# Six small loads move from SP's DMA queue to ACT's at the start of a one-core hybrid S5, DeltaNet and expert block

## The chip, the cores and the metric

The kernel runs on one core of a Trainium2 chip. Its time is the device time of one execution in microseconds (us), the median of several runs.

The engines that matter here are TensorE (PE in the rows, its weight loads PEld), VectorE (DVE), ScalarE (ACT), GpSimd (POOL) and SyncE (SP), which only issues DMAs. Each of them executes its own list of instructions in order. ACT issues DMAs as well, from the same list as its arithmetic. The issuing instructions have rows of their own, marked SPq or ACTq.

## What is computed

One block of a diffusion backbone, for 256 latent tokens `x` and 256 context tokens `ctx` of width 1024, in float32. In short:

```
mod   = silu(c) @ w_mod + b_mod          # the same with c_ctx for the context
h     = rmsnorm(x) * norm1 * (1 + scale) + shift
u, qkv, gate, b, a, br = split(h @ w_in)
yA    = S5(u)          # complex diagonal scan, lam_re, lam_im, log_step, b, c
yB    = GatedDeltaNet(silu(short_conv(qkv)), gate, b, a)
x     = x + gate1 * ((sig(br0) * yA @ w_a + sig(br1) * yB @ w_b) @ w_out)
x     = x + gate2 * experts(h2)          # top 4 of 32 clamped-SwiGLU experts, 12 MB each
out   = rmsnorm(x)
```

Of S5 the part that the change touches is the discretisation, which needs three short vectors:

```
dt  = exp(log_step);  mag = exp(lam_re * dt)
ar, ai = mag * cos(lam_im * dt), mag * sin(lam_im * dt)
fr, fi = ((ar - 1), ai) divided by (lam_re, lam_im)     # complex
bb  = (fr, fi) * (b_re, b_im)                            # complex
```

## The kernel before

**Order of the work.** SP is scheduled by hand: its DMAs stand in the order of the code. The order of the other engines' lists is found by a scheduler that simulates a timeline. So code that is moved changes those lists also far from its place.

**The start** (`front`, L143). `smalls` loads five short vectors (L138): `c` and `c_ctx` on SP, `norm1`, `gdn_conv` and `gdn_norm` on ACT. `load_x` loads x as three pieces of 1 MB in all (`xt`, L286) and ctx as two of 512 KB (`ct`, L274). `s5_load(0)` loads `lam_re`, `lam_im` and two halves of `log_step` into a tile `L` (L348 to L351). `mod1` computes `sc`, the SiLU of c and c_ctx, on ACT, and goes through eight blocks of 1 MB of w_mod (`wm`, L216), each with four products `ps<-wm,sc` on TensorE. `modrow` holds b_mod (L212) and gets the sum. `s5_load(1)` brings the four S5 matrices (`s5raw`, L356). Then follow the first blocks of w_in (`wba`, `win`).

**The norm and the modulation.** `load_h` squares the tokens on ACT (`junk`, with sums `ss`), takes the power -0.5 on GpSimd (`rs`, L334), scales on VectorE (`xn`, L300), transposes on TensorE (`ps<-ident,xn`) and copies to `hraw` on ACT. `mod1_end` transposes `modrow` and makes the shift `hsh` and the factor `ha` (L247, L248). `modulate` makes `h` from `hraw`, `ha` and `hsh`, on ACT for the context and on VectorE (L318) for the latent tokens. All of w_in needs `h`.

**The S5 vectors.** VectorE and ACT work on `L` (L378 to L404): Exp twice, Sin twice on ACT, the rest on VectorE, then powers `PW`, `PD` and a table `A` (L416 to L439). `BB` and `bbt` multiply `s5raw` by `L`. GpSimd builds `R` from `s5raw` and `PD`.

**The middle.** An order written out by hand alternates the projections of S5 and of the DeltaNet branch (`win` products of 512 columns), the short convolution, and the products `U,P` that drive the scan. The convolution of a head copies the projection to `raw`, starts `cacc` on ACT and adds four taps on VectorE (`cacc`, L685); then `cth` (tanh, ACT) and `kT` or `vT` (VectorE). `l2` squares `kT` on ACT (`sq`), sums it on TensorE (`ps<-ones,sq`), and makes `rnk` of it (L703 on VectorE, a power on GpSimd), which TensorE spreads over the partitions (`ps<-ident,rnk`). The S5 scan on VectorE takes `sct<-XC,A` and `XC<-XC,sct` in steps of falling width, for two directions. Behind that stand the triangular solve (`T`, through DRAM, from `KS`) and the DeltaNet scan, to about 434 us. From there on the experts' weights `w` stream (L1420).

**Completion semaphores.** The scheduler gives the DMAs of SP and ACT eight completion semaphores in turn, in the order in which it places them (`DMAHW0` to `DMAHW7` in the rows of order). A DMA waits until the one that had its semaphore before, eight places ahead, has landed.

Of the kernel before, what the change touches and what calls it, by code (L numbers as in the profile page):

```python
# [23 lines left out]
def dram(ap, off, dims):  # L24
    return bass.AP(tensor=ap.tensor, offset=ap.offset + off, ap=dims)


class Kern:
# [104 lines left out]
    def smalls(self):  # L133
        nc = self.nc
        self.col = {}
        for n, k in self.VECS:
            self.col[n] = self.w([128, k], "col_" + n)
            (nc.sync if n in ("c", "c_ctx") else nc.scalar).dma_start(self.col[n], dram(self.I[n], 0, [[k, 128], [1, k]]))  # L138
        self.gnh = self.w([128, 1], "gnh")
        nc.vector.tensor_scalar(self.gnh, self.col["gdn_norm"], 0.5, None, op0=OP.mult)  # L140

# [201 lines left out]
    def s5_load(self, part):  # L343
        nc, I = self.nc, self.I
        if part == 0:

            self.L = self.r("R2", "L")[:, :768].rearrange("p (a b) -> p a b", b=32)
            nc.sync.dma_start(self.L[:, 0], dram(I["s5_lam_re"], 0, [[32, 128], [1, 32]]))  # L348
            nc.sync.dma_start(self.L[:, 1], dram(I["s5_lam_im"], 0, [[32, 128], [1, 32]]))
            for a in range(2):  # L350
                nc.sync.dma_start(self.L[64 * a:64 * a + 64, 2], dram(I["s5_log_step"], 32 * a, [[0, 64], [1, 32]]))  # L351
            return

        self.raw = self.r("Q", "s5raw").rearrange("p (i x c) -> p i x c", i=4, c=16)
        for i, nm in enumerate(("s5_b_re", "s5_b_im", "s5_c_re", "s5_c_im")):
            nc.sync.dma_start(self.raw[:, i], dram(I[nm], 0, [[512, 128], [1, 512]]))  # L356
# [1394 lines left out]
def lay_w_in(np, a):  # L1751
# [10 lines left out]
    s5_lam_re=lambda np, a: a.reshape(32, 128).T,  # L1762
    s5_lam_im=lambda np, a: a.reshape(32, 128).T,
    s5_log_step=lambda np, a: a.reshape(32, 2).T,
# [24 lines left out]
```

## Time and profile before

| | us |
|---|---|
| median of 3 runs (1449.15 to 1454.15) | 1453.27 |
| the profiled execution | 1453.78 |
| its span in the trace | 1452.1 |
| busy: TensorE / VectorE / ACT / GpSimd | 1338.0 / 559.1 / 255.4 / 179.1 |

A busy time is the sum of an engine's instructions in the span. 473.06 MB are moved in it, most of them by the experts behind 434 us. The mean granted clock of TensorE is 0.97 of full speed.

### The profile page before, as it was taken

The numbers are of one execution on the slowest core, as the hardware profiler recorded it, in microseconds if no ns is written. First come the engines' busy times: TensorE is split into PE (matmuls) and PEld (weight loads), VectorE is DVE, ScalarE is ACT, GpSimd is POOL, SyncE is SP. The second block draws the span as 40 slices with busy tenths as digits, with TensorE's granted clock in tenths as the row PEclk, the third lists the DMA queues.
The fourth block names the chain that finished last, engine by engine and source line by source line (L and its number), as shares of the span: only waits on it lengthen the run. The fifth ranks groups of instructions, "written<-read, shape, count | busy, mean of one in ns | idle before, by whom it ended". The sixth has DMA issues, their size and how long they took to land. (4 is left out here: it accounts for less than half of the span.)

```text
span 1452.1 us, 18531 instructions
## 1 busy us (share of the span) xinstructions
PE 1338.0 (92%) x7469; PEld 600.9 (41%) x7469; DVE 559.1 (39%) x1083; ACT 255.4 (18%) x568; POOL 179.1 (12%) x299
## 2 busy tenths in 40 slices
PE   4799784999999899999999999999999999999985
PEld 1244362768787533333333333333333333333321
DVE  4977977664254403222322322232222222222213
ACT  3224321524301111011110110111011101111001
POOL 1921875111000100000000000000000000000000
PEclk9799896999999899999999999999999999999998
DMA  9464236711638899999999999999999999999994
GB/s 341 193 139 146 88 77 178 223 59 59 197 123 329 281 356 416 419 419 420 419 418 419 420 418 419 419 420 418 419 420 419 418 420 419 419 419 419 419 420 188
DMA packets 93275, 473.06 MB, mean 326 GB/s; under 512 B 24912, under 2 KB 29160, under 8 KB 41344
## 3 DMA queue, kind: packets, MB, share of 16 engines
q1 hardware_dynamic: 73216, 461.08, 79.4%
q10 hardware_dynamic: 19968, 10.73, 3.5%
q8 instruction: 61, 1.00, 0.3%
q14 instruction: 30, 0.25, 0.1%
HBM read 466.52 MB, written 3.16 MB: 323 GB/s over the span
## 5 line engine op out<-in xcount | busy, mean ns | idle before, releaser
L79 PE MATMUL ps<-w,xT 128*64 128x512 f32 x2048 | 485.7, 601 | 9.0 <-DMA w<-in_w_gate_up_dram 8.8
L79 PEld LDWEIGHTS ps<-w,xT 128*64 128x64 f32 x2048 | 137.6, 137 | 272.6 <-issue 241.8
L79 PE MATMUL ps<-w,aT 128*64 128x512 f32 x1024 | 233.1, 597 | 11.4 <-DMA w<-in_w_down_dram 11.1
L1725 DVE SCALAR_TENSOR_TENSOR od<-ps,cs,gt 128x512 f32<-128x512 f32 x31 | 23.3, 750 | 468.7 <-PE ps L79 468.7
L79 PEld LDWEIGHTS ps<-w,aT 128*64 128x64 f32 x1024 | 71.6, 137 | 165.5 <-issue 126.4
L94 DVE TENSOR_TENSOR x<-x,ps 128x512 f32<-128x512 f32 x128 | 84.1, 684 | 66.4 <-PE ps L79 66.4
L1506 POOL CAST selsd<-biad 128x128 fp32r<-128x128 f32 x32 | 9.4, 294 | 703.5 <-PE ps L79 703.5
L97 ACT ACTIVATE odh<-od 128x512 fp32r<-128x512 f32 x31 | 19.5, 629 | 427.0 <-DVE od L1725 427.0
L79 PE MATMUL ps<-h,win 128*128 128x512 f32 x192 | 91.3, 616 | 0.0
L79 PE MATMUL ps<-hx,wsp 128*128 128x256 f32 (+1 forms) x384 | 81.8, 360 | 0.0
L79 PEld LDWEIGHTS ps<-hx,wsp 128*128 128x128 f32 x384 | 62.9, 198 | 20.1 <-issue 9.8
L79 PE MATMUL ps<-h,oh 128*64 128x512 f32 x248 | 63.0, 604 | 0.0
L79 PEld LDWEIGHTS ps<-h,win 128*128 128x128 f32 x192 | 35.0, 195 | 47.6 <-issue 45.8
L97 ACT ACTIVATE sgm<-gt 128x512 f32<-128x512 f32 (+1 forms) x33 | 20.3, 618 | 163.6 <-DVE gt L1696 163.6
L79 PE MATMUL ps<-wm,sc 128*32 128x512 f32 x192 | 29.3, 699 | 20.2 <-DMA wm<-in_w_mod_dram 20.2
L97 ACT ACTIVATE aT<-ps 128x512 f32<-128x512 f32 (+1 forms) x33 | 19.3, 584 | 141.9 <-PE ps L83 141.9
L1696 DVE TENSOR_SCALAR gt<-ps 128x512 f32<-128x512 f32 (+1 forms) x33 | 22.2, 675 | 57.1 <-PE ps L79 57.1
L94 DVE TENSOR_TENSOR wsp<-win,wsp 128x512 fp32r<-128x512 f32 x48 | 32.0, 701 | 23.8 <-ACT wsp L97 23.5
L685 DVE SCALAR_TENSOR_TENSOR cacc<-raw,col_gdn_conv,cacc 128x512 f32<-128x512 f32 (+1 forms) x48 | 36.3, 756 | 5.5 <-ACT cacc L97 5.3
L1506 POOL CAST selsg<-biad 128x256 fp32r<-128x256 f32 x32 | 13.7, 427 | 190.7 <-PE ps L79 184.5
L97 ACT ACTIVATE wsp<-win 128x512 fp32r<-128x512 f32 x48 | 27.5, 624 | 49.2 <-PE ps L79 27.0
L79 PE MATMUL ps<-bias,selsg 128*128 128x512 f32 x64 | 28.6, 472 | 7.1 <-DVE ut L1698 6.6
(367 smaller groups left out, 1465.9 us busy)
## 6 DMA issues: line engine op xcount, KB each, us to landing
w<-in_w_gate_up_dram SPq DMA_DIRECT2D x242, 1024.0 KB
w<-in_w_down_dram SPq DMA_DIRECT2D x121, 1024.0 KB
wm<-in_w_mod_dram SPq DMA_DIRECT2D x24, 1024.0 KB
win<-in_w_in_dram SPq DMA_DIRECT2D x18, 1024.0 KB
w<-in_w_gate_up_dram SPq DMA_DIRECT2D x28, 512.0 KB
w<-in_w_down_dram SPq DMA_DIRECT2D x14, 512.0 KB
wo<-in_w_out_dram SPq DMA_DIRECT2D x4, 1024.0 KB
wa<-in_w_branch_a_dram SPq DMA_DIRECT2D x4, 512.0 KB
```

The source lines that it names most:

```text
L79: self.last = self.nc.tensor.matmul(out, lhsT, rhs, start=start, stop=stop, **kw)
L94: (eng or self.nc.vector).tensor_tensor(out, a, b, op=op)
L97: self.nc.scalar.activation(out, in_, func, **kw)
L685: nc.vector.scalar_tensor_tensor(acc[:, rows], rt[:, rows, k:k + 64], sc, acc[:, rows], op0=OP.mult, op1=OP.add)
L1506: nc.gpsimd.tensor_copy(v.rearrange("p (n s) -> p n s", s=CAP), dup[:, x:x + n, None].to_broadcast([128, n, CAP]))
L1696: V.tensor_scalar(g, z0, 7.0, None, op0=OP.min)
L1725: V.scalar_tensor_tensor(od, self.pd, self.cs, k.gt2, op0=OP.mult, op1=OP.mult)
```

## The change

`c` and `c_ctx` are loaded on ACT, ahead of the three vectors that were there, and so are the four loads of the S5 vectors. SP's list starts with x, ctx and w_mod.

```diff
         for n, k in self.VECS:
             self.col[n] = self.w([128, k], "col_" + n)
-            (nc.sync if n in ("c", "c_ctx") else nc.scalar).dma_start(self.col[n], dram(self.I[n], 0, [[k, 128], [1, k]]))
+            nc.scalar.dma_start(self.col[n], dram(self.I[n], 0, [[k, 128], [1, k]]))
...
-            nc.sync.dma_start(self.L[:, 0], dram(I["s5_lam_re"], 0, [[32, 128], [1, 32]]))
-            nc.sync.dma_start(self.L[:, 1], dram(I["s5_lam_im"], 0, [[32, 128], [1, 32]]))
+            nc.scalar.dma_start(self.L[:, 0], dram(I["s5_lam_re"], 0, [[32, 128], [1, 32]]))
+            nc.scalar.dma_start(self.L[:, 1], dram(I["s5_lam_im"], 0, [[32, 128], [1, 32]]))
             for a in range(2):
-                nc.sync.dma_start(self.L[64 * a:64 * a + 64, 2], dram(I["s5_log_step"], 32 * a, [[0, 64], [1, 32]]))
+                nc.scalar.dma_start(self.L[64 * a:64 * a + 64, 2], dram(I["s5_log_step"], 32 * a, [[0, 64], [1, 32]]))
```

SP's list is otherwise the same to its end. The lists of TensorE, VectorE, ACT and GpSimd are in another order at many places ahead of the experts.

The start of ACT's list, with the semaphores that each instruction waits for. `DMAHW0` is here that of `c` and then of `gdn_norm`, `DMAHW2` that of `c_ctx`, `DMAHW4` that of `norm1`, `DMAHW6` that of `gdn_conv`.

```order
+L138 DMA col_c<-in_c_dram 128x8
+L138 DMA col_c_ctx<-in_c_ctx_dram 128x8
 L138 DMA col_norm_94<-in_norm_dram 128x8
 L138 DMA col_gdn_conv<-in_gdn_conv_dram 128x60
-L138 DMA col_gdn_norm<-in_gdn_norm_dram 128x1
-L97 ACT_TABLE_LOAD [waits DMAHW1_49]
+L138 DMA col_gdn_norm<-in_gdn_norm_dram 128x1 [waits DMAHW0_49]
+L348 DMA L<-in_s_lam_re_dram 128x32 [waits DMAHW2_49]
+L349 DMA L<-in_s_lam_im_dram 128x32 [waits DMAHW4_49]
+L351 DMA L<-in_s_log_step_dram 64x32 [waits DMAHW6_49]
+L351 DMA L<-in_s_log_step_dram 64x32 [waits DMAHW0_49]
+L97 ACT_TABLE_LOAD
```

Six DMAs come into the list ahead of the first table load, and five of the DMAs there wait for an earlier landing, where before only the table load waited.

A little further on in ACT's list, the squares (`junk`), the functions on the S5 vectors (`L`) and the copies behind the transposes (`hraw`).

```order
-L97 ACT_TABLE_LOAD
-L97 ACTIVATE L<-L 128x32
-L97 ACTIVATE junk,ss<-xt 128x1024
-L97 ACTIVATE L<-L 128x32
-L97 ACTIVATE junk,ss<-xt 128x1024
+L97 ACTIVATE junk,ss<-ct 128x1024
+L97 ACTIVATE junk,ss<-xt 128x1024 x2
 L97 ACT_TABLE_LOAD
 L97 ACTIVATE L<-L 128x32 x2
 L97 ACTIVATE hraw_198<-ps 128x512 x4
+L97 ACT_TABLE_LOAD
+L97 ACTIVATE L<-L 128x32 x2
```

The squares now follow each other, and the two last functions on `L`, the Sin, stand behind the first four `hraw`, with a table load more. On TensorE the first sixteen transposes of `xn` stand behind three blocks of w_mod, where four of them stood behind the first block before. On VectorE `xn` stands ahead of the operations between Exp and Sin, and the last six operations on `A` stand behind the first `BB`, five of them ahead of `hsh`.

VectorE's list where the first v head's convolution (`raw_581`) and the S5 scan (`sct`, `XC`) meet.

```order
+L685 SCALAR_TENSOR_TENSOR cacc<-raw_581,col_gdn_conv,cacc 128x512 x4
 L94 TENSOR_TENSOR sct<-XC,A_334 128x512
 L94 TENSOR_TENSOR sct<-XC,A_334 128x16x16
-L94 TENSOR_TENSOR XC<-XC,sct 128x16x32
-L685 SCALAR_TENSOR_TENSOR cacc<-raw_581,col_gdn_conv,cacc 128x512
-L94 TENSOR_TENSOR XC<-XC,sct 128x16x32
-L685 SCALAR_TENSOR_TENSOR cacc<-raw_581,col_gdn_conv,cacc 128x512
+L94 TENSOR_TENSOR XC<-XC,sct 128x16x32 x2
 L94 TENSOR_TENSOR sct<-XC,A_334 128x256
 L94 TENSOR_TENSOR sct<-XC,A_334 128x8x16 x2
-L685 SCALAR_TENSOR_TENSOR cacc<-raw_581,col_gdn_conv,cacc 128x512
-L94 TENSOR_TENSOR XC<-XC,sct 128x8x32
```

The four `cacc` stood between the scan's steps (three of the four rows with a minus are seen here) and now stand together ahead of them. On TensorE the eight last `win` products of that head stand ahead of a block of products `U,P`, where one group of them stood behind it.

## Rows read from the trace of the kernel before

**Rows 1.** The head of the page

```profile
span 1452.1 us, 18531 instructions
```

**Rows 2.** Windows, expert part: busy us (count) per engine, PE clock, DMA share, GB/s

```profile
600.00:650.00 50.00, 50.00 (x227) 18.34 (x225) 14.38 (x26) 6.33 (x14) 1.09 (x3) 1.00 1.01 419
```

**Rows 3.** Timeline of SP's queue (start us, us, instruction, count)

```profile
0.81 0.39 SPq L138 DMA_DIRECT2D col_c<-in_c_dram  x1
...
1.71 1.69 SPq L286 DMA_DIRECT2D xt<-in_x_dram  x3
...
7.14 0.43 SPq L348 DMA_DIRECT2D L<-in_s_lam_re_dram  x1
...
9.39 5.37 SPq L216 DMA_DIRECT2D wm<-in_w_mod_dram  x8
...
434.87 30.76 SPq L1420 DMA_DIRECT2D w<-in_w_gate_up_dram  x11
```

**Rows 4.** Waits of SP's queue (total us, times, longest us)

```profile
SPq L274 <- DMA col_gdn_norm<-in_gdn_norm_dram: 2.6, 1, 2.6
```

**Rows 5.** Timeline of TensorE (in brackets: idle time before, releaser)

```profile
34.73 1.69 PE L79 MATMUL ps<-wm,sc 128*32 128x512 f32 x8 [1.47 <-DMA wm<-in_w_mod_dram]
...
44.66 1.89 PE L79 MATMUL ps<-h,wba 128*32 128x512 f32 x2 [5.63 <-DVE h L318]
...
141.67 2.13 PE L79 MATMUL ps<-U,P 128*64 128x64 f32 x64
...
162.32 1.87 PE L79 MATMUL ps<-ones,sq 128*128 128x1 f32 x8 [8.19 <-ACT sq L97]
...
190.51 2.05 PE L79 MATMUL ps<-ident,rnk 128*128 128x128 f32 x16 [0.17 <-POOL rnk L94]
```

**Rows 6.** Timeline of VectorE, first 50 us and the S5 scan

```profile
11.52 0.18 DVE L378 TENSOR_SCALAR L<-L 128x32 f32<-128x32 f32 x1 [4.60 <-DMA L<-in_s_lam_re_dram]
...
20.29 1.41 DVE L300 TENSOR_SCALAR xn<-xt,rs 128x1024 f32<-128x1024 f32 x2
...
29.40 0.19 DVE L94 TENSOR_TENSOR pwt<-A 128x32 f32<-128x32 f32 x1
...
30.30 0.24 DVE L433 TENSOR_SCALAR A<-A 128x160 f32<-128x160 f32 x1
35.37 1.29 DVE L94 TENSOR_TENSOR BB<-s5raw,L 128x512 f32<-128x512 f32 x2 [4.83 <-DMA s5raw<-in_s_b_re_dram]
36.58 0.69 DVE L94 TENSOR_TENSOR bbt<-s5raw,L 128x512 f32<-128x512 f32 x1
...
38.81 1.47 DVE L94 TENSOR_TENSOR bbt<-s5raw,L 128x512 f32<-128x512 f32 x1
...
41.71 0.15 DVE L247 COPY hsh<-ps 128x8 f32<-128x8 f32 x1
...
144.75 2.09 DVE L94 TENSOR_TENSOR sct<-XC,A 128x512 f32<-128x512 f32 x2 [6.07 <-ACT XC L97]
...
159.50 1.58 DVE L685 SCALAR_TENSOR_TENSOR cacc<-raw,col_gdn_conv,cacc 128x512 f32<-128x512 f32 x1
```

**Rows 7.** Waits of TensorE between 44 and 435 us

```profile
PE ps L79 <- DMA T<-KS: 25.0, 3, 15.2
```

**Rows 8.** Timeline of ACT, first 46 us and the S5 scan

```profile
2.53 1.28 ACT L97 ACT_TABLE_LOAD   x1 [2.53 <-DMA col_c<-in_c_dram]
...
9.94 1.06 ACT L97 ACTIVATE junk<-ct 128x1024 f32<-128x1024 f32 x1 [5.80 <-DMA lc<-in_b_router_dram]
...
18.20 0.35 ACT L97 ACTIVATE L<-L 128x32 f32<-128x32 f32 x2
24.90 4.03 ACT L97 ACTIVATE hraw<-ps 128x512 f32<-128x512 f32 x8 [6.35 <-PE ps L83]
...
161.12 0.63 ACT L97 ACTIVATE cth<-cacc 128x512 f32<-128x512 f32 x1 [14.74 <-DVE cacc L685]
```

**Rows 9.** Timeline of GpSimd, first 70 us

```profile
36.81 5.93 POOL L94 TENSOR_TENSOR R<-s5raw,PD 128x512 f32<-128x512 f32 x4 [0.21 <-DMA s5raw<-in_s_c_re_dram]
```

## The prediction

> **What bounds the kernel now.** I first read the page's head and the windows by stage. The span is 1452.1 us [rows 1]. Over the expert part TensorE is busy all the time, yet the DMA engines set the pace: a window of 50 us there shows a DMA share of 1.01 and 419 GB/s [rows 2], so 1 MB takes 1.05 / 0.419 = 2.5 us. The first eleven expert blocks are issued from 434.87 us on [rows 3], into buffers that the mixing part gives back. So the end of the program moves about one for one with the moment at which the mixing part ends, and what the change does has to be read ahead of 435 us. Nothing behind that is changed.
>
> Next I read the timeline of the first 50 us, engine by engine. SP issues c at 0.81, x from 1.71, then ctx, the S5 vectors from 7.14 and w_mod from 9.39 [rows 3]. The second ctx load waits 2.6 us for gdn_norm to land [rows 4], because a DMA waits for the one that used its completion semaphore before it. TensorE gets the eighth w_mod block at 34.73 [rows 5]. s5raw lands for VectorE at 35.37, after an idle time of 4.83 us; from there VectorE goes through BB, bbt, modrow and pt, and reaches hsh, with which h can start, at 41.71 [rows 6]. TensorE's products of the input projection start with h at 44.66, after 5.63 us idle [rows 5]. From the chain of waits, TensorE then waits little until 435 us: 8.19 us for sq at 162.32 [rows 5] and 25.0 us, in three waits, for T [rows 7].
>
> So there are two ways for the change to reach the end: h may start earlier or later, and the order that the scheduler writes anew may change a stall between 45 and 435 us.
>
> **The change, part by part.** *SP's issue.* c and c_ctx leave SP: x starts at 0.81 instead of 1.71, 0.90 us. The four S5 issues leave it: 9.39 - 7.14 = 2.25 us. That is 3.15 us of SP's own time [rows 3]. The 2.6 us wait of ctx does not simply go: its second load now waits for the first x block to land, and the first w_mod block for the second x block. The bytes that must land before the last w_mod block are the same. So the block of 34.73 comes earlier by at least the 0.90 us of the start and at most by 3.15 us. No row decides between them; I take the middle, 2.0 us: w_mod ends at 32.7, s5raw is there at 33.4.
>
> The Trainium skill, "DMA: Bandwidth & Descriptors", section "Issuing engines are not separate DMA queues", says that loads started by different engines run on the same 16 DMA engines and that starting them from several saves only the issuing time, usually little beside the transfer. [...]
>
> *What ACT's queue now does.* ACT executes in order, and its DMAs wait for semaphores too. In the rows of order, gdn_norm now waits for c, lam_re for c_ctx, lam_im for norm1, the first log_step load for gdn_conv and the second for gdn_norm. A small load that shares the engines with bulk lands late: lam_re was issued at 7.14 [rows 3] and used at 11.52 [rows 6], 4.4 us. c alone went out at 0.81 and was used at 2.53, 1.7 us [rows 3, 8]; beside x it will need between 1.7 and 4.4 us. So gdn_norm goes out at 2.5 to 5.2 and lands 4.4 us behind, at 6.9 to 9.6. With 8.0 the last log_step load goes out then, and the table load, 2.53 before, starts at about 8.5. Behind it stand the two sc (until 10.2, with 1.28 for the table load and 0.2 each), the modrow loads, of which the second waits for lam_im (1.7 + 4.4 + 4.4 = 10.5), and the squares, at about 11 instead of 9.94 [rows 8]. That sc is later is covered: it must be there for the first w_mod block, which lands seven blocks before the last, at 32.7 - 7 x 2.5 = 15.2. The table load and the two operations on L that stood between the squares are gone from there, so the four (1.06 us each [rows 8], taken as 1.15 with the read of their sum) end at about 16, where they ended a table load ahead of Sin, at 18.20 - 1.28 = 16.9. If each landing takes a us longer, they end 2 us later.
>
> *The S5 vectors' arithmetic.* The Exp on L stood between the squares and the Sin behind them, at 18.20 [rows 8]. Now all of it stands behind the squares, and Sin also behind four of the eight hraw and a further table load (1.28 us). hraw needs the transposes, and these now stand behind three w_mod blocks: the third lands at 32.7 - 5 x 2.5 = 20.2, its products take 1 us (the last block's took 1.69 [rows 5], in a slower stretch), the first transposes 0.6 by estimate, four hraw 2.0 (half of 4.03 [rows 8]), the table load until 25.1, Sin until 25.5 instead of 18.55. VectorE's chain from Sin to the end of A ran from 18.55 to 30.54, of which xn took some 2.7 us (two pairs like the one of 1.41 us at 20.29, a little overlapped) [rows 6, 8]: 9.3 us. Its last six operations, from 29.40 to 30.54 or 1.1 us [rows 6], are moved behind BB. So BB may begin at 25.5 + 8.2 = 33.7. s5raw would be there at 33.4. The chain on VectorE had 4.83 us to spare; after the change it has none, and is what is late next: of the 2.0 us that the loads gain, 35.37 - 33.7 = 1.7 us arrive at BB.
>
> *From BB to h.* Before, 41.71 - 35.37 = 6.34 us. Five A operations moved in between add 0.9 us. GpSimd's R starts at 36.81 [rows 9], when s5raw's third part has landed, and beside it VectorE's product bbt takes 1.47 us instead of 0.69 [rows 6]. R will start 2.0 us earlier, at 34.8, so 1.1 us behind BB instead of 1.44: 0.34 us of work that ran undisturbed is slowed by the same factor, 0.4 us more. hsh then comes at 33.7 + 6.34 + 0.9 + 0.4 = 41.3, against 41.71: **-0.4 us**. Bounds: -2.0 if the chain is in time, nothing is slowed and the A operations fit into gaps; +2.9 if the four operations of this kind before hsh are all slowed (4 x 0.78 = 3.1 us), A comes on top (0.9) and BB gains 1.1.
>
> *The reordered middle.* Of the first v head (raw_581 in the rows of order) the four cacc stood between the steps of the S5 scan on VectorE, the last at 159.50 for 1.58 us [rows 6]; cth on ACT waits 14.74 us for it, with sq queued behind [rows 8], and TensorE 8.19 us for sq. Now the four stand together ahead of the scan, so sq is ready in time. But VectorE has the same work to do, and TensorE soon needs rnk, which VectorE reaches only behind the second half of the scan: ident,rnk at 190.51 already waits 0.17 us [rows 5]. So the stall moves there, less what VectorE itself gains. VectorE idled 6.07 us until 144.75 for XC [rows 6]. The last products of this head's projection now stand ahead of a block of 64 products U,P, which took 2.13 us from 141.67 [rows 5]; with them cacc starts about that much earlier, inside the idle time: -2.1 us, and I take **-2.1**. Bounds: 0 (if XC becomes late by as much) and -8.2 (if rnk is no limit). The rows of K and T stand as before, so their 25.0 us [rows 7] stay.
>
> *Sum.* The profiled execution took 1453.78 us (1452.1 of span, 1.7 around it): 1453.78 - 0.4 - 2.1 = 1451.3. It lay 0.5 us above the median of the three runs, 1453.27, so beside that median 1450.8. A change of 0.5%, 7.3 us, is about what a measurement of this kernel can tell from none.
>
> **The rivals.** *Everything arrives* (chance 0.20): the loads' 2.0 us reach h and the whole stall of 8.19 us goes: -10.2 us from the median, 1443.1. For it: TensorE is busy elsewhere between 45 and 190 us. Against it: the chain's spare time is gone, and rnk is waited for already.
>
> *It is hidden* (0.16): TensorE's start is set by VectorE, the middle by VectorE's scan, both with the same work, so nothing arrives: 1453.3. For it: nothing that TensorE waits for between 45 and 190 us is a load that moved. The rule of the Trainium skill named above comes out here where the issue is off the path.
>
> *Slower* (0.14): the series of landings on ACT. If a small load beside x and ctx takes 8.8 us, twice the row, c lands at 9.6, gdn_norm at 18.4, the last log_step load goes out then, the squares run from 20.6 to 25.7, xn ends at 29.7, Sin at 34.0, BB starts at 42.2 and hsh comes at 42.2 + 7.6 = 49.8: +8.1 us, and if the middle gives nothing back 1461.4. Each us of a landing counts twice, so from 8.4 us per landing on it is slower by over 0.5%. Against it: lam_re took 4.4 us with 2 MB of x and ctx in flight ahead of it.
>
> **How the numbers follow.** The forecast, with 0.50, is the sum, 1450.8; its own range goes from the loads' full gain, 1449.2, to its first term's upper bound with nothing from the second, 1456.2. Faster by over 0.5% is the first rival, 0.20; slower is the third, 0.14; the forecast and the second rival lie within 0.5%, 0.66. The range over all reaches to the first rival, and towards the third as far as a landing of 7.2 us (+5.7): 1443 to 1459.
>
> **What the profile would show.** Right: x on SP at 0.81; ACT's first table load near 8.5; squares ending near 16; Sin near 25; the last w_mod products from 32.7; BB near 34 with little or no wait for s5raw; hsh near 41; TensorE's wait for sq gone and a new one of some 6 us for rnk; the first expert block issued near 432. Wrong: BB waiting over 1 us for s5raw (the chain was not late); sq's wait gone without one at rnk (first rival); a first table load after 12 us (third rival); another DMA rate in the expert part, since then the end does not follow the mixing part.

## The result and the profile after

The changed kernel takes 1467.55 us (median of 4 runs, 1464.68 to 1471.19), the kernel before 1452.87 us in the same session (4 runs, 1449.15 to 1454.15). The ratio is 1.0107, with a 95% interval of [1.0076, 1.0138]: slower by 14.7 us. The forecast was 1450.8 us, and the time lies outside the range of 1443 to 1459. The profiled execution of the changed kernel took 1464.68 us, the least of its four; beside that of before, 1453.78, it is 10.9 us longer. That difference is the one that the two traces can explain.

Head of the page and the window of the expert part, for the changed kernel (columns as in [rows 2]).

```profile
span 1462.9 us, 18532 instructions
```

```profile
600.00:650.00 50.00, 50.00 (x225) 18.51 (x226) 12.08 (x22) 6.33 (x14) 1.17 (x4) 1.00 1.01 419
```

The span grew by 10.8 us, and the expert part still runs at 419 GB/s, as in [rows 2]. So the loss lies ahead of the experts, as in the reading of the kernel before. SP's queue says how much of it had come about by then.

```profile
0.80 1.65 SPq L286 DMA_DIRECT2D xt<-in_x_dram  x3
...
6.21 12.58 SPq L216 DMA_DIRECT2D wm<-in_w_mod_dram  x8
...
446.15 19.20 SPq L1420 DMA_DIRECT2D w<-in_w_gate_up_dram  x8
```

w_mod is issued 3.2 us earlier than in [rows 3], the first expert block 446.15 - 434.87 = 11.3 us later. TensorE's timeline in the changed kernel:

```profile
28.55 3.00 PE L79 MATMUL ps<-wm,sc 128*32 128x512 f32 x24
48.09 1.11 PE L83 MATMUL ps<-ident,modrow 128*128 128x128 f32 x4 [16.55 <-DVE modrow L94]
54.46 1.89 PE L79 MATMUL ps<-h,wba 128*32 128x512 f32 x2 [5.25 <-ACT h L97]
...
171.66 1.05 PE L79 MATMUL ps<-ones,sq 128*128 128x1 f32 x8
...
207.34 3.78 PE L79 MATMUL ps<-ident,rnk 128*128 128x128 f32 x16 [8.69 <-POOL rnk L94]
```

The last three w_mod blocks go through without a pause and end at 31.55, where the last one alone began at 34.73 before [rows 5]. So the loads are early. Then TensorE stands still for 16.55 us, for `modrow`, which VectorE has to finish. The first product with h comes at 54.46 against 44.66 [rows 5], 9.8 us late. Those 9.8 are nearly all of the 11.3. VectorE's timeline shows where they arise.

```profile
27.82 0.42 DVE L94 TENSOR_TENSOR L<-L 128x32 f32<-128x32 f32 x3 [2.50 <-ACT L L97]
...
32.06 0.30 DVE L438 COPY PD<-PW 128x144 f32<-128x144 f32 x1
...
32.69 1.09 DVE L94 TENSOR_TENSOR A<-A 128x32 f32<-128x32 f32 x1
33.70 0.17 DVE L429 COPY A<-PW 128x32 f32<-128x32 f32 x1
33.78 0.29 DVE L438 COPY PD<-PW 128x144 f32<-128x144 f32 x1
...
34.79 0.18 DVE L94 TENSOR_TENSOR A<-A 128x32 f32<-128x32 f32 x1
...
36.01 1.02 DVE L94 TENSOR_TENSOR pwt<-A 128x32 f32<-128x32 f32 x1
36.96 1.13 DVE L94 TENSOR_TENSOR A<-A 128x32 f32<-128x32 f32 x1
38.01 1.13 DVE L94 TENSOR_TENSOR A<-A,pwt 128x32 f32<-128x32 f32 x1
...
44.35 0.18 DVE L94 TENSOR_TENSOR A<-A,pwt 128x32 f32<-128x32 f32 x1
...
45.35 1.29 DVE L94 TENSOR_TENSOR BB<-s5raw,L 128x512 f32<-128x512 f32 x2
...
47.35 0.68 DVE L94 TENSOR_TENSOR modrow<-modrow,ps 128x512 f32<-128x512 f32 x1
...
49.39 1.59 DVE L94 TENSOR_TENSOR pt<-BB,PD 128x512 f32<-128x512 f32 x1
50.90 1.08 DVE L94 TENSOR_TENSOR A<-A,pwt 128x32 f32<-128x32 f32 x1
51.90 0.15 DVE L247 COPY hsh<-ps 128x8 f32<-128x8 f32 x1
```

And GpSimd's in the same stretch:

```profile
32.61 4.38 POOL L94 TENSOR_TENSOR R<-s5raw,PD 128x512 f32<-128x512 f32 x4 [0.86 <-DVE PD L439]
36.95 1.09 POOL L94 TENSOR_TENSOR rtmp<-s5raw,PD 128x512 f32<-128x512 f32 x1
38.01 1.09 POOL L94 TENSOR_TENSOR R<-s5raw,PD 128x512 f32<-128x512 f32 x1
...
42.23 2.15 POOL L94 TENSOR_TENSOR R<-s5raw,PD 128x512 f32<-128x512 f32 x2
48.82 3.11 POOL L94 TENSOR_TENSOR pto<-BB,PD 128x512 f32<-128x512 f32 x2 [4.45 <-DVE BB L94]
```

Read the two together. An operation on A has 32 elements a partition and takes 0.19 us [rows 6]. From 32.61 GpSimd works on R, in products of 1.09 us back to back, until 44.38: eleven products. In just that time eleven operations on A take 1.02 to 1.13 us each (one of them 0.67), one for each product, and their ends keep step with GpSimd's: the one begun at 36.96 ends at 38.09, and the R product of 36.95 at 38.04. One operation, at 34.79, slips through with 0.18 just as one product ends and the next begins. When GpSimd stops at 44.38, A is back at 0.18. The two copies at 33.70 and 33.78, which read one tensor, keep their 0.17 and 0.29 in the midst of it. The eleven lose 9.5 us in all (each row less 0.18 or 0.19). BB, which waited for s5raw before, starts at 45.35 with no wait at all, and hsh comes 10.2 us later than in [rows 6].

That A and R meet has two causes. Before, A was done at 30.54 and R began at 36.81 [rows 6, 9]. Now R begins at 32.61, released by `PD`, because s5raw is early; and A is late, because Sin is. ACT's timeline:

```profile
5.00 0.33 ACTq L138 DMA_DIRECT2D col_gdn_norm<-in_gdn_norm_dram  x1
...
10.73 1.28 ACT L97 ACT_TABLE_LOAD   x1 [10.73 <-DMA L<-in_s_lam_re_dram]
...
13.93 1.06 ACT L97 ACTIVATE junk<-ct 128x1024 f32<-128x1024 f32 x1 [1.59 <-DMA L<-in_s_lam_im_dram]
...
26.27 1.28 ACT L97 ACT_TABLE_LOAD   x1
27.56 0.35 ACT L97 ACTIVATE L<-L 128x32 f32<-128x32 f32 x2
```

The first table load stands at 10.73 (2.53 before [rows 8]), behind nine DMAs of which five wait for landings; the squares start 4.0 us later; and Sin ends at 27.91, not 18.55.

### The profile page after: what moved, and what is told of

Same layout as the page of the kernel before. It is cut to its first block, busy times and chain, and to the rows that moved or that the text cites. A ratio compares the mean times of both kernels' runs of the same rounds, so it can differ in the third digit from the quotient of the medians.

```text
span 1462.9 us, 18532 instructions
## 1 busy us (share of the span) xinstructions
PE 1337.5 (91%) x7469; PEld 600.6 (41%) x7469; DVE 564.0 (39%) x1083; ACT 254.9 (17%) x568; POOL 174.1 (12%) x299
## 5 line engine op out<-in xcount | busy, mean ns | idle before, releaser
L79 PE MATMUL ps<-hx,wsp 128*128 128x512 f32 (+1 forms) x384 | 81.9, 359 | 0.7 <-ACT wsp L97 0.7
L79 PE MATMUL ps<-wm,sc 128*32 128x512 f32 x192 | 33.5, 693 | 14.2 <-DMA wm<-in_w_mod_dram 14.1
L685 DVE SCALAR_TENSOR_TENSOR cacc<-raw,col_gdn_conv,cacc 128x512 f32<-128x512 f32 (+1 forms) x48 | 33.7, 703 | 13.9 <-ACT cacc L97 13.4
L79 PE MATMUL ps<-odh,ST 64*128 64x512 f32 x124 | 32.5, 497 | 2.9 <-ACT odh L97 1.6
```

The source lines that it names most:

```text
L79: self.last = self.nc.tensor.matmul(out, lhsT, rhs, start=start, stop=stop, **kw)
L685: nc.vector.scalar_tensor_tensor(acc[:, rows], rt[:, rows, k:k + 64], sc, acc[:, rows], op0=OP.mult, op1=OP.add)
```

## The experiments

Theory: each two-input operation of VectorE beside GpSimd's R waits until the R product under way ends, so the loss is A meeting R. Rival one: the chain is late through ACT's queue alone, and R does not matter. Rival two: the scheduler's new order of the middle costs the time. (In the first expectations these are theories A, B and C.) Each kernel is set against the kernel before on the same chip; "changed" is the change of this document.

**e1: the changed kernel with R kept behind A.** PD is allocated ahead of A's powers, and A's scratch is laid into it, so that PD, and with it R, comes behind A. The work is the same.

```diff
+        PD = self.w([128, 2, 2, 9, 16], "PD", "s1")
+        q4 = lambda c, n: self.A8[:, c, n].rearrange("p (c d g) -> p c d g", c=2, d=2)
         for n in range(4):
-            self.cmul(self.A8[:, 0, n + 1], self.A8[:, 1, n + 1], self.A8[:, 0, n], self.A8[:, 1, n],
-                      self.A8[:, 0, n], self.A8[:, 1, n], tmp[:, 0])
+            self.cmul(q4(0, n + 1), q4(1, n + 1), q4(0, n), q4(1, n), q4(0, n), q4(1, n), PD[:, :, :, 0, :8])
...
-        PD = self.w([128, 2, 2, 9, 16], "PD", "s1")
```

> The changed kernel, with one thing else: the table A is computed with its scratch laid into the tile PD, so that PD is filled, and GpSimd's R can start, only when A is done. Nothing is added or left out. Theory A (the loss comes from VectorE's small operations on A running beside GpSimd's R, each of them 1.0 to 1.1 us instead of 0.19): A's 24 operations take about 4 us again, BB starts near 36 instead of 45.4, hsh near 42 instead of 51.9, and the time falls by about 10 us, to 1455 to 1460. Theory B (the small loads and the arithmetic of ACT behind them are late, and that is the loss): Sin stays at 27.6, so hsh comes no more than 2 us earlier and the time stays at 1464 to 1469. Theory C (the order of the middle costs it): no change of more than 3 us.

Measured: 1455.51 us (10 runs, 1453.47 to 1460.98), ratio 1.0028 [1.0011, 1.0046]. Of the 1.07% that the change cost, 0.79% is gone. VectorE and GpSimd in e1:

```profile
38.03 0.18 DVE L94 TENSOR_TENSOR A<-A 128x32 f32<-128x32 f32 x1
38.14 0.19 DVE L94 TENSOR_TENSOR A<-A,PD 128x32 f32<-128x32 f32 x1
...
40.05 1.28 DVE L94 TENSOR_TENSOR BB<-s5raw,L 128x512 f32<-128x512 f32 x2
...
45.36 0.15 DVE L247 COPY hsh<-ps 128x8 f32<-128x8 f32 x1
```

```profile
43.79 5.62 POOL L94 TENSOR_TENSOR R<-s5raw,PD 128x512 f32<-128x512 f32 x4 [7.55 <-DVE PD L438]
```

A runs at 0.18 and 0.19 throughout, and BB comes 3.4 us behind the first of these operations, at 36.68, where it was 12.7 us behind in the changed kernel. The profiled run is one of the longer ones, 1460.54 us; in it Sin is at 31.94, another 4.4 us late, and hsh still earlier than after the change. Against the kernel before, Sin is 13.7 us late here and hsh 3.65 us, while in the changed kernel they are 9.4 and 10.2 us late. So the lateness of Sin alone costs the smaller part, and rival one falls as the main cause. Rival two does not explain the changed kernel's 9.8 us either, since they are there before the middle begins.

**e2: the kernel before, made to meet R.** SP's queue stays as it was but for two of the four S5 matrices, c_re and c_im, which go ahead of w_mod. No load is moved to ACT.

```diff
         self.s5_load(0)
+        self.s5_load(2)
         self.mod1()
...
         for i, nm in enumerate(("s5_b_re", "s5_b_im", "s5_c_re", "s5_c_im")):
-            nc.sync.dma_start(self.raw[:, i], dram(I[nm], 0, [[512, 128], [1, 512]]))
+            if (i > 1) == (part == 2):
+                nc.sync.dma_start(self.raw[:, i], dram(I[nm], 0, [[512, 128], [1, 512]]))
```

> The kernel before, all small loads on their old queues; only the two halves of s5raw that GpSimd's R reads (s5_c_re, s5_c_im, 0.5 MB) are loaded ahead of w_mod, the other two stay behind it. Theory A: R now starts when PD is there, near 27, beside the operations on A, which stretch to about 1.05 us each while R runs; BB starts at 43 to 50 instead of 35.4, hsh some 8 to 14 us later, and the time is 1460 to 1468 although nothing was moved between queues. Theory B: the S5 chain is as early as before and has 4.8 us to spare, w_mod is 1.3 us later: 1452 to 1456.

Measured: 1470.08 us (4 runs, 1469.4 to 1471.35), ratio 1.0122 [1.0102, 1.0142]. Its GpSimd and VectorE:

```profile
26.22 3.29 POOL L94 TENSOR_TENSOR rtmp<-s5raw,PD 128x512 f32<-128x512 f32 x3 [8.37 <-DVE PD L441]
```

```profile
28.53 1.03 DVE L94 TENSOR_TENSOR pwt<-A 128x32 f32<-128x32 f32 x1
29.48 1.13 DVE L94 TENSOR_TENSOR A<-A 128x32 f32<-128x32 f32 x1
...
52.08 0.15 DVE L248 COPY hsh<-ps 128x8 f32<-128x8 f32 x1
```

Sin is at 17.76 here, as early as ever, and yet hsh comes at 52.08, as late as after the change. GpSimd executes 18 products and sums of R by 46.14, and 18 operations on A are slow; the three beside sums of 1.26 to 1.28 us take 1.30 to 1.31. So R, beginning beside A, makes a loss of the same size without the change. A small part of it is another's: 0.5 MB now stands ahead of w_mod, whose last block TensorE takes at 36.67, 1.9 us later than before; but TensorE then waits 11.64 us for `modrow`, so it is VectorE that holds up h. The time is 2 us above the expected 1460 to 1468.

**e8: the changed kernel with R's products cut in halves.** The same elements in twice the instructions. It was run once.

```diff
             def times(out, c, reim):
-                self.tt(out, self.bc(c[:, h]), self.pw(d, reim, s0, hb), OP.mult, eng)
+                x, y = self.bc(c[:, h]), self.pw(d, reim, s0, hb)
+                for u in (slice(0, 2), slice(2, 4)):
+                    self.tt(out[:, u], x[:, u], y[:, u], OP.mult, eng)
```

> The changed kernel with each product of R on GpSimd cut into two of half the size (256 columns instead of 512). The order of all engines differs, so the time tells little; what counts are the durations of the operations on A beside R. If an operation of VectorE waits until the operation of GpSimd that is under way has ended, it takes about half as long as in the changed kernel, 0.5 to 0.7 us instead of 1.02 to 1.13. If both share a path at a lower rate, its time does not hang on the length of GpSimd's operation and stays near 1.05.

Measured: 1462.95 us, one run. GpSimd and VectorE:

```profile
33.26 4.89 POOL L94 TENSOR_TENSOR R<-s5raw,PD 128x256 f32<-128x256 f32 x8 [0.65 <-DVE PD L438]
```

```profile
34.64 0.57 DVE L94 TENSOR_TENSOR pwt<-A 128x32 f32<-128x32 f32 x1
35.12 0.68 DVE L94 TENSOR_TENSOR A<-A 128x32 f32<-128x32 f32 x1
...
43.03 1.28 DVE L94 TENSOR_TENSOR BB<-s5raw,L 128x512 f32<-128x512 f32 x2
```

An R product now takes 4.89 / 8 = 0.61 us, and an operation on A beside it 0.57 to 0.68, where it was 1.02 to 1.13 beside products of 1.09. A rate shared between the engines would have left it near 1.05. So the price is a wait for one GpSimd instruction for each VectorE instruction. In the changed kernel it was the same 0.9 us for 512 elements a partition as for 32: beside `pto`, `pt` took 1.59 us where such a product alone takes 0.69, and an operation on A 1.08 instead of 0.18. Beside the larger ones GpSimd is held up too: R's products took 5.93 / 4 = 1.48 us before [rows 9] and 1.09 beside A. BB came only 2.3 us earlier in e8, because shorter waits let more of A's operations fall into R's time: 16 of the 19 ahead of BB pay the smaller price, where 11 paid the larger.

**e9: the layout of e1 in the kernel before**, a control for e1's edit.

> The kernel before with the edit of e1_pd_behind_a, as a check on that edit: A's scratch lies in PD. There A was done 5 us before R's data came, so nothing is to be gained; TensorE's order is the same as before. Theory A: 1450 to 1455, no difference. If the edit itself were worth something, it would show here, and e1 would say less.

Measured: 1452.33 us (10 runs, 1448.06 to 1458.54), ratio 0.9987 [0.9973, 1.0]. The edit by itself gives nothing that could be e1's 0.79%. (The profiled execution is the longest of the ten, 1458.54 us.)

**e3 and e4: each half of the change alone.** e3 moves only c and c_ctx to ACT, e4 only the four S5 loads.

```diff
-            (nc.sync if n in ("c", "c_ctx") else nc.scalar).dma_start(self.col[n], dram(self.I[n], 0, [[k, 128], [1, k]]))
+            nc.scalar.dma_start(self.col[n], dram(self.I[n], 0, [[k, 128], [1, k]]))
```

> Half of the change: c and c_ctx on ACT, the S5 vectors stay on SP. In its order the Sin stand ahead of all hraw and A is done ahead of BB. Theory A: Sin near 20, A done near 33, before R's data lands near 35, so no stretch: 1449 to 1456. Theory B: gdn_norm waits for c, and with it ACT's arithmetic is 1 to 3 us later: 1454 to 1458. Theory C: by the order of the middle, which differs little from that of before, within 3 us of it.

> The other half: the four S5 loads on ACT, c and c_ctx stay on SP. The last log_step load waits for gdn_norm's lane neighbours and three loads in a row wait for landings; Sin stands ahead of all hraw. Theory A: Sin near 21 to 23, A done at 33 to 35, R's data near 34: at most a few operations are stretched, 1450 to 1457. Theory B: this half has the waits on landings, so it keeps most of the loss: 1461 to 1468.

Measured: e3 1452.46 us (10 runs, 1450.18 to 1460.89), ratio 0.9998 [0.9977, 1.002]; e4 1458.41 us (10 runs, 1452.31 to 1461.57), ratio 1.0031 [1.0015, 1.0046]. In neither do A and R meet, and neither shows the loss of the whole. e3 came as expected; e4 lies between its two expected ranges. In e4 the front even gains, as VectorE's and TensorE's rows show:

```profile
33.97 1.29 DVE L94 TENSOR_TENSOR BB<-s5raw,L 128x512 f32<-128x512 f32 x2 [3.02 <-DMA s5raw<-in_s_b_re_dram]
```

```profile
42.96 1.88 PE L79 MATMUL ps<-h,wba 128*32 128x512 f32 x2 [5.92 <-DVE h L318]
...
64.28 1.11 PE L83 MATMUL ps<-ident,pt 128*128 128x128 f32 x4 [4.56 <-DVE pt L94]
```

h is 1.7 us early, but a new wait of 4.56 us for `pt` follows, and the first expert block goes out at 434.86, no earlier than before and no later. So e4's 0.3% does not come from A and R; and of the 4.4 us by which its profiled span is longer none has arisen when the experts begin.

**e5, e6 and e7: R held off by late loads.** s5_c_re and s5_c_im are issued behind the first w_in blocks: in the changed kernel (e5), in the kernel before (e6), and in the changed kernel with the S5 vectors put first on ACT (e7).

```diff
             self.win_load()
+        self.s5_load_c()
         self.load_h()
...
```

> The changed kernel; only the two parts of s5raw that R reads (s5_c_re, s5_c_im) are loaded behind the first w_in blocks, some 8 us later. In its order ACT's and VectorE's first lists are those of the changed kernel, and GpSimd first takes two products that read BB. Theory A: nothing of GpSimd runs beside the operations on A, these take 0.19 us again, BB starts near 36 instead of 45.4, hsh near 41, and the time is 1451 to 1458. Theory B (lateness of ACT's loads and arithmetic): Sin stays near 27 and the time stays at 1464 to 1470.

> The kernel before, small loads on their old queues, with the same delay of s5_c_re and s5_c_im: the opposite of the run that loads them early. Theory A, carried on: R beside BB, bbt and pt costs the kernel before something too; hsh comes at 39.5 to 40.5 instead of 41.7 and h is made at less than 1.1 us apiece, so TensorE's first h product comes 2 to 3 us earlier and the time is 1449 to 1452. Rival: R is 8 us later and the S5 products of the middle wait for it: 1454 to 1460.

> The changed kernel with the S5 vectors ahead of c on ACT's queue, so that none of the four waits for a landing, and with s5_c late as above. In its order the Sin stand ahead of all hraw, as before the change. Theory A: Sin near 20 to 22, A done by 33, BB when s5raw lands (near 33), hsh near 38 to 39; TensorE's first h product at 42 to 43 instead of 44.7: 1448 to 1454. If what is left of the loss in the other runs (about 4 us with the S5 vectors on ACT) comes from the order of the middle, it shows again as waits of TensorE for pt near 65 us, and the time is 1453 to 1458.

| | median us (runs) | ratio to before |
|---|---|---|
| e5 | 1462.41 (7) | 1.0054 [1.0034, 1.0075] |
| e6 | 1457.34 (10) | 1.0026 [1.0009, 1.0043] |
| e7 | 1461.93 (4) | 1.006 [1.0038, 1.0083] |

None of the three came into theory A's range; e6 lies in its rival's. In e5 A runs at 0.18 to 0.19 again, but for one operation beside a later product of GpSimd, BB starts at 36.88 and h's first product at 45.98, only 1.3 us later than before. Yet the first expert block goes out at 444.70, 9.8 us later: TensorE waits 14.24 us for `sq` at 172.54. In e6 h's first product is 2.5 us early, at 42.18, and the first expert block at 434.98 is not. In e7 no operation on A is slow, but Sin is at 25.26, not at the expected 20 to 22, and h's first product comes at 44.98, no earlier than before. So a front that is mended need not arrive. Here the middle is in a new order and R is later too (its first product at 46.89, 44.18 and 46.98, not at 36.81); which of the two costs e5 its front, no run separates.

**e10 to e12: a better kernel?** R in halves in the kernel before (e10), with R's sums halved too (e11), and the same with c and c_ctx on ACT (e12).

> The kernel before with R's products on GpSimd cut in two (256 columns each), sums not cut. VectorE then waits half as long whenever it meets R: beside BB to h, and in the S5 scan beside the second R. Theory A: bbt near 1.0 us instead of 1.47, hsh 0.5 to 1.5 us earlier, scan steps of 128x128 and smaller near 0.6 to 0.8 us instead of 1.2; the time is 1446 to 1452. Rival: the new order of the middle is worth more than that either way, as in the runs so far (-4 to +8 us there): 1449 to 1461.

> As the run before, and the sums of R cut in two as well. Theory A: the scan of the first direction, 28 us before, gets 3 to 8 us shorter, and the wait of TensorE for sq with it: 1444 to 1452. Rival: as there, 1449 to 1461.

> c and c_ctx on ACT (the half of the change that cost nothing) with all of R cut in two. Theory A: within 2 us of the run before. A large difference between the two would be the order of the middle alone.

Measured, 10 runs each: e10 1451.41 us, 0.999 [0.9976, 1.0003]; e11 1453.84, 1.0002 [0.9988, 1.0016]; e12 1455.2, 1.0019 [0.9996, 1.0042]. All three start h's products earlier (42.22, 42.16 and 43.23 against 44.66), and none is measurably faster; e11 missed the 1444 to 1452 of theory A. No version of this study beats the kernel before.

## Why the prediction was wrong

**What bounds the kernel.** Right: 419 GB/s in the expert part as before, and an issue of the first expert block that is 11.3 us late beside a span that is 10.8 us longer.

**SP's issue.** Right in direction, too small in size. The forecast gave the last w_mod block 2.0 us, at most 3.15. It was read by TensorE at about 30.55 (two thirds into the 24 products of 28.55), 4.2 us earlier than 34.73, and it had landed by then. The bound counted SP's own time alone. The wait of 2.6 us on gdn_norm [rows 4] is gone from SP's queue, where ctx now waits 1.6 us for x; which part of the gain that is was not separated.

**ACT's queue.** Right in kind, 2.4 us short. gdn_norm went out at 5.00, inside the forecast's 2.5 to 5.2, but the load that waits for its landing, the last of log_step, went out at 10.22 and not 8.0. So the first table load came at 10.73 and not 8.5, the squares ran from 13.93 to 18.87 and not from 11 to 16, and Sin ended at 27.91 and not 25.5.

**The step that failed** is "So BB may begin at 25.5 + 8.2 = 33.7" under *The S5 vectors' arithmetic*, with the paragraph on R behind it. BB began at 45.35. The chain was priced at the rate that it had in the trace of before, where it ran with GpSimd idle: 8.2 us from Sin's end to BB, which became 17.4. The prediction had seen what R does to VectorE, 1.47 us for 0.69, but it took that as a factor, and put it only on the four products behind BB. By its own numbers A ended 1.1 us before R (33.7 and 34.8). Sin came 2.4 us later than forecast and R 2.2 us earlier, so A and R met; and from there the loss grew by itself, since each operation on A that waits keeps the next one inside R's time. e1 takes the meeting away and 0.79% goes; e2 brings it about in the kernel before and 1.22% comes. The upper bound of the term, +2.9, had the same flaw: it slowed four products and no small operation. Even the five operations on A that the forecast itself had beside R, behind BB, stood there at their undisturbed 0.9 us together.

The row of 1.47 for 0.69 could not tell a factor from a wait, for one operation of that size beside one R product fits both. The operations on A can: as a factor of 1.47 / 0.69 = 2.1 they would take 0.40 us, by a wait about 1.1, and the trace shows 1.02 to 1.13.

The Trainium skill has this rule, in "SBUF — State Buffer", sections "SBUF: two separate sides" and "Who interferes with whom": VectorE and GpSimd share one pair of ports, which is locked for a whole instruction, against a VectorE operation with two inputs from SBUF too where GpSimd's reads SBUF, and the other engine blocks until it is free. The trace agrees: the waits end with R's products, and halved products halve them (e8). The copies beside R, with one input, passed at 0.17 and 0.29 us.

**From BB to h.** 51.90 - 45.35 = 6.55 us against 7.6 forecast. R was over by then, so bbt took 0.69; one product beside `pto` took 1.59 and the operation on A behind it 1.08.

**The reordered middle.** Half right. The wait for sq is gone and one of 8.69 us for rnk has come, as forecast (some 6). The -2.1 us is not there. The cacc were to start earlier, inside VectorE's idle time. In the trace they do not:

```profile
159.07 3.84 DVE L685 SCALAR_TENSOR_TENSOR cacc<-raw,col_gdn_conv,cacc 128x512 f32<-128x512 f32 x4 [4.40 <-ACT cacc L97]
162.84 2.83 DVE L94 TENSOR_TENSOR sct<-XC,A 128x512 f32<-128x512 f32 x2
```

The scan's first step begins at 162.84, 18.1 us later than at 144.75 [rows 6]; 9.8 of that is h's delay. cacc now makes the scan wait, where it had stood between the scan's steps, and VectorE still idles 4.40 us ahead of it. A wait of 6.3 us for `cth` has come too, and those for `pt` are 5.3 us, not 2.6. Further on a part came back: TensorE's waits for T are 15.9 us, not 25.0 [rows 7]. From h to the first expert block the changed kernel loses 11.3 - 9.8 = 1.5 us in all, less than two executions with the same order there differ by (see below).

**The rivals.** The third, "slower", has the right sign and not its mechanism: it needed 8.4 us per landing, and a first table load behind 12 us; gdn_norm's wait for c was over at 5.00, and the table load stood at 10.73. Nothing in the list of rivals had VectorE slowed by GpSimd ahead of BB.

**What stays open.** e1 and e4 are both about 0.3% slower than before though A and R do not meet there. Single profiles cannot say why. Against the kernel before, the stretch between h and the first expert block changes by -1.5 us in e1, +1.7 in e4, -4.0 in e3, +8.5 in e5, +2.6 in e6, +4.4 in e7, -2.2 in e10 and +3.0 in e9. A new order of the middle is not needed for such differences: in e3 and e9 TensorE, VectorE, ACT and GpSimd execute the same instructions there in the same order as in the kernel before, and yet the stretch is 4.0 us shorter in one and 3.0 us longer in the other. Behind the first expert block's issue, too, the profiled executions take between 1016.8 us (changed kernel) and 1021.6 us (e4). So rival two is neither shown nor excluded as the source of some 0.3%, and only e5's +8.5 is clear of these differences. What arises ahead of h is: its first product comes at 44.66, 44.47 and 44.01 us in the kernel before, e3 and e9, against 54.46 and 55.20 in the changed kernel and e2. Of the changed kernel's 14.7 us the trace accounts for 10.9; the rest lies in executions that were not profiled and is not explained.

## What to carry to other kernels

Where GpSimd works through long two-input products, as here, a chain of small two-input operations on VectorE costs there about the number of its instructions times one GpSimd instruction, as long as both last; price it so as soon as the two may overlap, and keep them apart by data (e1) or by where the loads stand. When a change makes one chain later and lets another start earlier, compare the distance between the two, not only the ends of each. And a load on a computing engine's queue delays that engine's arithmetic by the landings that the load has to wait for: here six small DMAs put the first table load from 2.53 to 10.73 us.

## What was not expected of the hardware

Two operations of the same form on VectorE, 128x32 with two inputs, took 0.18 us and 1.13 us, by whether they met a product of GpSimd; a copy in the same microseconds did not change. Halving GpSimd's products brought the wait to 0.57 to 0.68 us and lengthened GpSimd's work by a tenth (2 x 0.61 = 1.22 us for 1.09). In e10 the step from BB to hsh took 5.57 us instead of 6.34 and began 0.8 us earlier; h's first product was 2.4 us early, and yet the whole stayed within the measurement's uncertainty.
